# A two-block transformer kernel: the delta rule's triangular inverse by doubling block sizes on TensorE, and the recurrences issued in small steps

## The chip, the cores and the metric

The kernel runs on one core of a Trainium2 chip. The metric is device time in microseconds (us) of one execution. A core has TensorE (matrix products), VectorE (DVE), ScalarE (ACT) and GpSimd (POOL), which each work through a queue of their own in order, and SyncE (SP), whose queue here issues most DMAs. They wait for each other by semaphores.

## The reference

Input x is 1024 tokens of width 1024, in float32. Two blocks follow each other.

The first block has adaptive normalisation, a spatial gating unit beside top-k sparse attention, and a feed-forward of width 4096. The second projects its normalised input to `z` (the delta rule's features), `u` and gates, and then joins two recurrences and another such feed-forward:

```python
z = xn @ w_in[l]
z_rwkv, u, gates = jnp.split(z, [SHIFT_COLS, SHIFT_COLS + SSM_WIDTH], axis=-1)
z_mix = z_rwkv + (token_shift(z_rwkv) - z_rwkv) * mu_shift[l]
y_a = rwkv7_time_mix(z_mix, ...)      # the delta rule, 8 heads of 64
y_b = s5_ssm(u, ...)                  # S5: a complex diagonal state per group
g_a, g_b = jnp.split(jax.nn.sigmoid(gates), 2, axis=-1)
x = x + (g_a * y_a + g_b * y_b) @ w_out[l]
x = x + sq_relu_mlp(rmsnorm(x, norm2_g[l]), w_ff_up[l], w_ff_down[l])
```

The delta rule is a scan over tokens of a 64x64 state for each head:

```python
sk = jnp.einsum('bhvk,bhk->bhv', state, kk_t)
state = (state * w_t[:, :, None, :]
         - sk[..., None] * b_t[:, :, None, :]
         + v_t[..., None] * k_t[:, :, None, :])
y_t = jnp.einsum('bhvk,bhk->bhv', state, r_t)
```

The kernel computes it in chunks of 64 tokens. Within a chunk the effect of the tokens on each other is a strictly triangular 64x64 matrix for each head, and the chunk needs the inverse of one plus this matrix. That inverse is the subject of the change.

## The kernel before

**Dense products.** Every large product keeps float32 accuracy by splitting both operands into a high and a low part: `mm3` issues three matmuls of 128x512 (L66, L68, L69; called dense products below). After the first of them it calls `next(self.weave, None)`, so that a generator hung there emits one of its steps between the matmuls. Weights come through `load_w`: a 512 KB DMA on SP's queue into `wraw`, a cast by ACT and a subtraction by POOL into `whl`.

**Stages.** The sequence is worked in two halves of 512 tokens. For each, `sequences(h, ...)` computes the second block's input projection (`in2`) over 4352 columns, among it the delta rule for four tiles of 128 tokens (`rwkv(tt)`, two chunks of 64 tokens and eight heads each). In the first half the first block's feed-forward for the second half of the tokens comes next, then `merge`, which reads S5's and the delta rule's results back from DRAM (`yin`) and multiplies them by `w_glu` and `w_rwkv_proj`. In the second half seven eighths of the first half's last feed-forward stand between `sequences` and `merge`.

**The delta rule's tile.** `rwkv(tt)` loads its features (zw, zk, zr, zv), forms decays with two small products (L1271, L1272), normalises the keys (L1296), and forms the 64x64 matrices MM (L1326). Before the change it then inverts 32x32 blocks: MM's blocks go to DRAM (`lt_d`) and come back as L with one block on each partition, 31 steps of two VectorE operations (L1387 and L1389) run the substitution, the result goes through DRAM again (`tt_d`) into TT, VectorE transposes it (TI, L1401), and two small products (L1405, L1411) join two 32x32 inverses to one of 64x64. Products with the inverse (L1422) and with the state (L1436 to L1471) follow, a normalisation (L1483 to L1491), four transposes (L128), the gate G, and a store to `y_d`.

**S5.** `s5_steps(h)` is a generator: input products (L1721), rotations and scans on VectorE (up to L1736), copies to `s5t`, output products (L1764 and L1766) with weights of its own from DRAM (`s5w`), `y` by ACT (L1769) and a store to `y_d`. In the first half it hangs on `weave` in the last blocks of the first feed-forward, in the second in `in2`.

**The order.** A scheduler simulates a timeline and puts each engine's instructions into an order that is fixed when the kernel is built. Its priorities follow the order in which the code emits them; what stands in `with self.urgent()` goes ahead. In the kernel before, a delta tile is emitted whole, between two parts of `in2`.

Of the kernel before, what the change touches and what calls it, by code (L numbers as in the profile page):

```python
# [34 lines left out]
class Kernel:  # L35
# [64 lines left out]
    def load_w(self, w, k0, nk, c0, n, spare=None):  # L100
# [18 lines left out]
        return [(hl[:, 0, k, :], hl[:, 1, k, :]) for k in range(nk)]  # L119

# [741 lines left out]
    def ffn(self, hT, w_up, w_down, blocks=range(8), acc=None, gain=None, weave=None, spare=None):  # L862
# [6 lines left out]
        for fb in blocks:  # L869
            if fb == 5 and weave:  # L870
                next(weave)
            if fb == 6 and weave:
                self.weave = weave
# [44 lines left out]
        if weave:  # L918
            for _ in weave:
                pass  # L920
        return G, acc, ss

    def sequences(self, h, xT, s5=None):

        if h:
            self.in2(h, xT, 1792, 2304, True)
            s5 = self.s5_steps(h)
            next(s5)
            self.in2(h, xT, 0, 768)
# [27 lines left out]
    def run(self):  # L957
# [132 lines left out]
        after = self.ffn(hT, I["w_ff1"][0], I["w_ff2"][0], gain="G2", weave=self.s5_steps(0))  # L1090
# [79 lines left out]
    def rwkv_setup(self):  # L1170
# [55 lines left out]
    def rwkv(self, tt):  # L1226
# [18 lines left out]
        def ps512():  # L1245
            return self.tp.tile([P, 512], F32, name="tp")
# [624 lines left out]
```

## Time and profile before

| | before |
|---|---|
| median of 3 runs | 3047.42 us (3038.46 to 3047.6) |
| profiled execution, its own time | 3063.16 us |
| its span, first to last instruction | 3061.4 us |
| TensorE busy | 2831.0 us (92%) |
| VectorE, ACT, POOL busy | 1745.7, 1245.3, 1460.9 us |
| mean granted TensorE clock | 0.96 |

Times inside the execution count from the span's start. A busy time is the sum of an engine's instructions, overlaps counted once. The granted clock is 1.00 at TensorE's upper level (2.4 GHz) and 0.5 at its lower (1.2 GHz); a stretch's figure is the mean. An idle stretch of an engine is put down to what released the instruction that ended it. The length that a matmul's row shows is a modelled end, so its cost within a stream is read from the distance between starts.

### The profile page before, as it was taken

The numbers are of one execution on the slowest core, as the hardware profiler recorded it, in microseconds if no ns is written. First come the engines' busy times: TensorE is split into PE (matmuls) and PEld (weight loads), VectorE is DVE, ScalarE is ACT, GpSimd is POOL, SyncE is SP. The second block draws the span as 40 slices with busy tenths as digits, with TensorE's granted clock in tenths as the row PEclk, the third lists the DMA queues.
The fourth block names the chain that finished last, engine by engine and source line by source line (L and its number), as shares of the span: only waits on it lengthen the run. The fifth ranks groups of instructions, "written<-read, shape, count | busy, mean of one in ns | idle before, by whom it ended". The sixth has DMA issues, their size and how long they took to land.

```text
span 3061.4 us, 42378 instructions
## 1 busy us (share of the span) xinstructions
PE 2831.0 (92%) x15600; PEld 2337.1 (76%) x15600; DVE 1745.7 (57%) x3752; ACT 1245.3 (41%) x2121; POOL 1460.9 (48%) x1285
## 2 busy tenths in 40 slices
PE   6977998999998899889989999998899999999998
PEld 5865776787887777667777888887777778888887
DVE  5699569999946944445563563433655634332122
ACT  4545555444455333343333443332433333433333
POOL 4665544544445743434433465443343435454444
PEclk9988999999999999899999999999999999999999
DMA  7445332222224555333225484653323235442232
GB/s 252 136 130 178 124 118 64 90 79 69 73 84 148 179 164 152 103 86 90 76 84 147 147 274 123 178 147 107 81 92 90 82 90 155 141 131 97 97 97 83
DMA packets 301504, 370.22 MB, mean 121 GB/s; under 512 B 70936, under 2 KB 209902, under 8 KB 301040
## 3 DMA queue, kind: packets, MB, share of 16 engines
q1 hardware_dynamic: 293296, 351.75, 37.9%
q10 hardware_dynamic: 8000, 15.76, 1.5%
q8 instruction: 123, 2.02, 0.3%
q14 instruction: 85, 0.70, 0.1%
HBM read 315.80 MB, written 51.65 MB: 120 GB/s over the span
## 4 chain that ended last, share of the span: by engine, by line
PE 57%; DVE 27%; DMA 8%; issue 3%; ACT 2%; SPq 2%; POOL 1%; ACTq 0%; POOLq 0%; DVEq 0%
PE mm L66 16%; PE mm L68 16%; PE mm L69 16%; DVE junk L669 4%; DMA L<-lt_d 3%; DVE T L1389 2%; DVE Ttmp L1387 2%; DVE topk L680 2%; PE tp L128 1%; DVE acc L902 1%; DVE score L643 1%; DVE p L746 1%; DMA TT<-tt_d 1%; DVE p L735 1%; PE tp L764 1%
## 5 line engine op out<-in xcount | busy, mean ns | idle before, releaser
L118 POOL TENSOR_TENSOR whl<-wraw,whl 128x512 fp32r<-128x512 f32 (+1 forms) x836 | 1134.7, 1382 | 1255.7 <-ACT whl L116 1187.1
L66 PE MATMUL mm<-hT,whl 128*128 128x512 f32 x1760 | 699.1, 398 | 21.6 <-DVE acc L902 13.5
L68 PE MATMUL mm<-hT,whl 128*128 128x512 f32 x1760 | 701.6, 400 | 0.0
L69 PE MATMUL mm<-hT,whl 128*128 128x512 f32 x1760 | 694.8, 397 | 3.9 <-POOL whl L118 3.9
L116 ACT CAST whl<-wraw 128x1024 fp32r<-128x1024 f32 (+1 forms) x418 | 435.1, 1042 | 541.5 <-PE mm L69 389.7
L66 PE MATMUL mm<-whl,hT 128*128 128x512 f32 (+1 forms) x1584 | 614.6, 402 | 42.9 <-DVE acc L902 18.5
L68 PE MATMUL mm<-whl,hT 128*128 128x512 f32 (+1 forms) x1584 | 625.6, 396 | 0.4 <-POOL whl L118 0.4
L69 PE MATMUL mm<-whl,hT 128*128 128x512 f32 (+1 forms) x1584 | 614.3, 396 | 0.9 <-DVE hT L61 0.9
L66 PEld LDWEIGHTS mm<-hT,whl 128*128 128x128 f32 x1760 | 336.1, 191 | 97.2 <-DVE acc L902 15.2
L69 PEld LDWEIGHTS mm<-hT,whl 128*128 128x128 f32 x1760 | 336.3, 191 | 73.7 <-POOL whl L118 5.0
L66 PEld LDWEIGHTS mm<-whl,hT 128*128 128x128 f32 x1584 | 305.2, 193 | 112.2 <-DVE acc L902 22.2
L68 PEld LDWEIGHTS mm<-hT,whl 128*128 128x128 f32 x1760 | 336.1, 191 | 66.3 <-issue 0.9
L68 PEld LDWEIGHTS mm<-whl,hT 128*128 128x128 f32 x1584 | 305.9, 193 | 60.7 <-issue 1.2
L69 PEld LDWEIGHTS mm<-whl,hT 128*128 128x128 f32 x1584 | 303.3, 192 | 62.2 <-DVE hT L61 1.8
L902 DVE TENSOR_TENSOR acc<-mm,acc 128x512 f32<-128x512 f32 x240 | 160.6, 686 | 189.2 <-PE mm L69 188.7
L61 DVE TENSOR_TENSOR hT<-sm,hT 128x512 fp32r<-128x512 f32 x112 | 94.4, 846 | 265.2 <-ACT hT L60 264.5
L881 ACT ACTIVATE sm<-mm 128x512 f32<-128x512 f32 x128 | 76.5, 598 | 273.1 <-PE mm L69 267.3
L669 DVE TENSOR_SCALAR_CACHE_REDUCE junk<-score,topk 128x640 uint8<-128x640 f32 (+4 forms) x192 | 179.5, 941 | 1.8
L1387 DVE TENSOR_TENSOR Ttmp<-L,T 128x60 f32<-128x60 f32 (+24 forms) x248 | 77.8, 314 | 95.5 <-DMA L<-lt_d 88.1
L60 ACT CAST hT<-sm 128x512 fp32r<-128x512 f32 x144 | 89.3, 620 | 31.0 <-DVE sm L1835 28.3
L764 PE MATMUL tp<-pT,vhl 128*128 128x256 f32 x288 | 64.1, 310 | 25.0 <-ACT pT L760 7.4
L743 ACT ACTIVATE p<-p,nm 128x128 f32<-128x128 f32 (+7 forms) x64 | 49.6, 778 | 91.4 <-DVE nm L739 60.5
(470 smaller groups left out, 3489.2 us busy)
## 6 DMA issues: line engine op xcount, KB each, us to landing
wraw<-w_ff SPq DMA_DIRECT2D x128, 512.0 KB
wraw<-w_in SPq DMA_DIRECT2D x100, 512.0 KB
wraw<-w_ff_up SPq DMA_DIRECT2D x64, 512.0 KB
wraw<-w_ff_down SPq DMA_DIRECT2D x64, 512.0 KB
wraw<-w_ada SPq DMA_DIRECT2D x32, 512.0 KB
wraw<-w_out SPq DMA_DIRECT2D x32, 512.0 KB
raw<-w_ada SPq DMA_DIRECT2D x16, 512.0 KB
x_d<-acc ACTq DMA_DIRECT2D x16, 512.0 KB
```

The lines of the kernel that those rows point to most:

```text
L60: self.nc.scalar.copy(hi, src)
L61: (engine or self.nc.gpsimd).tensor_tensor(lo, src, hi.bitcast(F32), op=OP.subtract)
L66: nc.tensor.matmul(ps, a[0], b[0], start=start, stop=False)
L68: nc.tensor.matmul(ps, a[0], b[1], start=False, stop=False)
L69: nc.tensor.matmul(ps, a[1], b[0], start=False, stop=stop)
L116: nc.scalar.copy(hl[:, 0], raw)
L118: nc.gpsimd.tensor_tensor(hl[:, 1, s], raw[:, s], hl[:, 0, s].bitcast(F32), op=OP.subtract)
L669: V.tensor_scalar(junk[:, :n], sel, value, 0.0, op0=op, op1=OP.add, accum_out=cnt)
L764: nc.tensor.matmul(o, self.vhl[(s0 + i) // 4][:, (s0 + i) % 4, kv, :], t[:, x, 256 * i:256 * i + 256], start=(s0 + i + x == 0), stop=(s0 + ...
L881: nc.scalar.activation(r, ps, AF.Relu)
L902: nc.vector.tensor_tensor(d, pss[j], d, op=OP.add)
L1387: V.tensor_tensor(tmp[:, :n, :w], L[:, j:j + 1, j + 1:].to_broadcast([P, n, w]), T[:, :n, j:j + 1].to_broadcast([P, n, w]), op=OP.mult)
```

## The change

The inverse is no longer done by substitution. Masks `joins` for the block widths 1, 2, 4, ... 32 are built once. Starting from inverses of 2x2 blocks, five doublings each compute Y = MM times S, masked to the blocks that are joined, and then S (the inverse so far) and its transpose St by two further products, `each` being sixteen 64x64x64 products, one for each head and chunk. VectorE takes Y out of PSUM with the mask, ACT copies S and St. Both DRAM bounces and TI go.

`rwkv` becomes a generator with `yield` between its steps, and `delta(h)` chains the four tiles. It hangs on `weave`, ahead of S5 in the first half: `in2` from column 1792 (2304 in the second half) and the feed-forward behind it emit one step at each dense product. S5 of the second half now hangs on all of `in2` up to column 1792, and `drain` emits what is left before the merge.

The diff, cut to its core (most of the added `yield` lines are left out, they stand between the groups of instructions of `rwkv` that the listing above shows; line numbers of the kernel after are 5 higher here up to the delta rule and up to 30 higher behind it):

```diff
                 nc.gpsimd.tensor_tensor(hl[:, 1, s], raw[:, s], hl[:, 0, s].bitcast(F32), op=OP.subtract)
         return [(hl[:, 0, k, :], hl[:, 1, k, :]) for k in range(nk)]
+
+    def drain(self):
+
+        for _ in self.weave:
+            pass
...
-    def ffn(self, hT, w_up, w_down, blocks=range(8), acc=None, gain=None, weave=None, spare=None):
+    def ffn(self, hT, w_up, w_down, blocks=range(8), acc=None, gain=None, spare=None):
...
         for fb in blocks:
-            if fb == 5 and weave:
-                next(weave)
-            if fb == 6 and weave:
...
                     down(0, jj)
                     down(1, jj)
-        if weave:
-            for _ in weave:
-                pass
         return G, acc, ss
 
-    def sequences(self, h, xT, s5=None):
-
-        if h:
-            self.in2(h, xT, 1792, 2304, True)
-            s5 = self.s5_steps(h)
-            next(s5)
-            self.in2(h, xT, 0, 768)
-            self.weave = s5
-            self.in2(h, xT, 768, 1792)
-            for _ in s5:
-                pass
-        else:
-            self.in2(h, xT, 0, 1024, True)
-            self.weave = s5
-            self.in2(h, xT, 1024, 1792)
-            for _ in s5:
-                pass
+    def sequences(self, h, xT, s5):
+
+
+        self.in2(h, xT, *((1792, 2304) if h else (0, 512)), True)
+        self.weave = s5
+        self.in2(h, xT, *((0, 1792) if h else (512, 1792)))
+        self.drain()
+        self.weave = chain(self.delta(h), iter(()) if h else self.s5_steps(0))
+        self.in2(h, xT, 2304 if h else 1792, 4352)
+
+    def delta(self, h):
         with ExitStack() as st:
             self.rwkv_pools(st)
             for tt in range(4 * h, 4 * h + 4):
-                self.rwkv(tt)
-        self.in2(h, xT, 2304 if h else 1792, 4352)
+                yield from self.rwkv(tt)
 
 
...
@@ -1087,7 +1078,8 @@
         self.residual(1, None, rows, ss, lambda tt: I["x"][0, tt * P:(tt + 1) * P, :])
         self.sequences(0, xT, s5)
         *_, hT = self.norm_T(self.scaled_rows(rows, rstd=self.ssx_rstd(1)), self.s2, self.sh2)
-        after = self.ffn(hT, I["w_ff1"][0], I["w_ff2"][0], gain="G2", weave=self.s5_steps(0))
+        after = self.ffn(hT, I["w_ff1"][0], I["w_ff2"][0], gain="G2")
+        self.drain()
         ys = self.merge_in(0)
         self.residual(1, *after, lambda tt: self.x_d[tt], False)
         mT = self.merge(0, *ys)
...
-        self.sequences(1, xT)
+        self.sequences(1, xT, self.s5_steps(1))
         *_, hA = hA
         w = I["w_ff_up_2"][0], I["w_ff_down_2"][0]
         self.ffn(hA, *w, range(7), os)
+        self.drain()
...
-        self.eye32 = c.tile([P, 8, 32], F32, name="eye32")
-        nc.gpsimd.memset(self.eye32, 0.0)
-        for g in range(4):
-            nc.gpsimd.affine_select(self.eye32[32 * g:32 * g + 32], self.eye32[32 * g:32 * g + 32],
-                                    pattern=[[-4, 8], [1, 32]], compare_op=OP.not_equal, fill=-1.0, base=-g,
-                                    channel_multiplier=0)
+
+        self.joins = c.tile([P, 7, 64], F32, name="joins")
+        nc.gpsimd.memset(self.joins, 0.0)
+        for ch in range(2):
+            q = self.joins[64 * ch:64 * ch + 64]
+            for x in range(6):
+                w = 1 << x
...
+            up = q[:, 6].rearrange("p (b u) -> p b u", u=2)[:, :, 1:2]
+            nc.gpsimd.affine_select(up, up, pattern=[[-2, 32], [0, 1]], compare_op=OP.not_equal, fill=1.0, base=0,
+                                    channel_multiplier=1)
+        nc.vector.tensor_tensor(self.joins, self.joins, self.eye2[:, None].to_broadcast([P, 7, 64]), op=OP.add)
         self.state = self.stp.tile([P, 4, 64], F32, name="state")
         nc.vector.memset(self.state, 0.0)
-        self.lt_d = [self.dram.tile([32, 32, 32], F32, name=f"lt_d{t}") for t in range(8)]
-        self.tt_d = [self.dram.tile([32, 8, 4, 32], F32, name=f"tt_d{t}") for t in range(8)]
 
     def rwkv_pools(self, st):
         self.rk = self.pool("rk", st=st)
         self.ew = self.pool("ew", 4, st=st)
         self.TT = self.rk.tile([P, 8, P], F32, name="TT")
         self.nc.vector.memset(self.TT, 0.0)
-        self.TI = self.rk.tile([P, 8, 32], F32, name="TI")
-        self.nc.vector.memset(self.TI, 0.0)
 
...
@@ -1326,15 +1334,29 @@
                     nc.tensor.matmul(ps[:, c], BK[r, hh // 2, 2 * c:2 * c + 2, :].rearrange("p x t -> p (x t)"),
                                      PR[r, :, hh // 2, 64 * c:64 * c + 64], start=True, stop=True)
                 V.tensor_tensor(MM[:, hh + e], ps, self.mask2[:, None].to_broadcast([P, 2, 2, 64]), op=OP.mult)
-
-        lt = rk.tile([P, 8, 32], F32, name="ltc")
-        for b in range(4):
-            r = slice(32 * b, 32 * b + 32)
-            V.tensor_copy(lt[r], MM[r, :, b // 2, 0, 32 * (b % 2):32 * (b % 2) + 32])
-        for b in range(4):
-            nc.sync.dma_start(self.lt_d[tt][8 * b:8 * b + 8].rearrange("h j i -> j h i"), lt[32 * b:32 * b + 32])
-        L = rk.tile([P, 32, 32], F32, name="L")
-        nc.sync.dma_start(L, self.lt_d[tt].rearrange("b j i -> b (j i)")[None].to_broadcast([4, 32, 1024]))
+            yield from range(2)
+
+
+        S, St, Y = (rk.tile([P, 8, 64], F32, name=n) for n in ("S", "St", "Y"))
+
+        def join(x):
+            return self.joins[:, x, None, :].to_broadcast([P, 8, 64])
+
+        def each(ps, a, b):
+
+            for i in range(8):
+                for c, q in chunks:
+                    nc.tensor.matmul(ps[q, i * 64:i * 64 + 64], a[c][q, i], b[q, i], start=True, stop=True)
+
+        M = [MM[:, :, c, 0, :] for c in range(2)]
+        eye = self.eye2[:, None, :].to_broadcast([P, 8, 64])
+        for c, q in chunks:
+            V.tensor_tensor(M[c][q], M[c][q], eye[q], op=OP.subtract)
+        for c, q in chunks:
+            V.tensor_tensor(St[q], M[c][q], join(6)[q], op=OP.mult)
+        ps = ps512()
+        each(ps, M, eye)
+        V.tensor_tensor(S, ps.rearrange("p (h d) -> p h d", h=8), join(0), op=OP.mult)
 
         PQ = rk.tile([P, 8, 2, 64], F32, name="PQ")
...
@@ -1377,42 +1403,25 @@
         V.tensor_tensor(W, W, bc(self.lnb), op=OP.add)
         V.tensor_tensor(W, W, k4(pg), op=OP.mult)
         V.tensor_tensor(G1, k4(pg), bc(self.lnw), op=OP.mult)
-
-        T = rk.tile([P, 8, 32], F32, name="T")
-        tmp = rk.tile([P, 8, 32], F32, name="Ttmp")
-        nc.gpsimd.tensor_copy(T, self.eye32)
-        for j in range(31):
-            n = j // 4 + 1
-            w = 31 - j
-            V.tensor_tensor(tmp[:, :n, :w], L[:, j:j + 1, j + 1:].to_broadcast([P, n, w]),
-                            T[:, :n, j:j + 1].to_broadcast([P, n, w]), op=OP.mult)
-            V.tensor_tensor(T[:, :n, j + 1:], T[:, :n, j + 1:], tmp[:, :n, :w], op=OP.subtract)
-        for cg in range(4):
-            nc.sync.dma_start(self.tt_d[tt][:, :, cg, :], T[32 * cg:32 * cg + 32])
-        TT, TI = self.TT, self.TI
-        for c in range(2):
-            nc.gpsimd.memset(TT[64 * c:64 * c + 32, :, 64 * c + 32:64 * c + 64], 0.0)
-        for r in range(4):
-            nc.sync.dma_start(TT[32 * r:32 * r + 32, :, 32 * r:32 * r + 32],
-                              self.tt_d[tt][8 * r:8 * r + 8].rearrange("h m g i -> (m g) h i"))
-
-        for c in range(2):
-            r = slice(64 * c, 64 * c + 32)
-            V.transpose(TI[r], TT[r, :, 64 * c:64 * c + 32])
-        pz = ps512()
-        for i in range(8):
-            for c, q in chunks:
-                nc.tensor.matmul(pz[q, i * 32:i * 32 + 32], MM[q, i, c, 0, :], TI[q, i, :], start=True, stop=True)
-        Z = rk.tile([P, 8, 32], F32, name="Z")
-        nc.scalar.copy(Z, pz[:, :256].rearrange("p (h j) -> p h j", h=8))
-        po = ps512()
-        for i in range(8):
-            for c, q in chunks:
-                nc.tensor.matmul(po[64 * c:64 * c + 32, i * 32:i * 32 + 32], Z[q, i, :], TT[q, i, 64 * c + 32:64 * c + 64],
-                                 start=True, stop=True)
-        for c in range(2):
-            r = slice(64 * c, 64 * c + 32)
-            nc.scalar.copy(TT[r, :, 64 * c + 32:64 * c + 64], po[r, :256].rearrange("p (h i) -> p h i", h=8))
+        yield from range(2)
+
+        TT = self.TT
+        for x in range(1, 6):
+            ps = ps512()
+            each(ps, M, S)
+            V.tensor_tensor(Y, ps.rearrange("p (h d) -> p h d", h=8), join(x), op=OP.mult)
+            yield from range(3)
+            ps, pst = ps512(), ps512()
+            each(pst, (Y, Y), St)
+            pst = pst.rearrange("p (h d) -> p h d", h=8)
+            if x < 5:
+                each(ps, (St, St), Y)
+                nc.scalar.copy(S, ps.rearrange("p (h d) -> p h d", h=8))
+                nc.scalar.copy(St, pst)
+            else:
+                for c, q in chunks:
+                    nc.scalar.copy(TT[q, :, q], pst[q])
+            yield from range(3)
 
         X = rk.tile([P, 8, 64], F32, name="X")
         for hg in range(2):
...
+        yield from range(8)
         po = ps512()
         for kt in range(4):
...
+        yield from range(12)
         for kt in range(4):
             TO = self.s5_w(self.toep_d[:, 8 * kt:8 * kt + 8])
             OU = self.s5_w(self.out_d[:, 8 * kt:8 * kt + 8])
```

What it moves, first on TensorE in one tile of the delta rule. Before (`TI`, `TT`, `Z` are the tiles of the old join, `mm` rows are dense products):

```order
L69 MATMUL mm<-hT,whl 128x512
L66 MATMUL mm<-hT,whl 128x512
L68 MATMUL mm<-hT,whl 128x512
L1405 MATMUL tp<-TI,MM 64x32 x16
L69 MATMUL mm<-hT,whl 128x512
...
L1411 MATMUL tp<-TT,Z 32x32 x16
L69 MATMUL mm<-hT,whl 128x512
```

The same place after (L1349 is `each`):

```order
L1397 MATMUL tp<-zw,wgu 128x128 x4
L1400 MATMUL tp<-zr,blk 128x512
L1349 MATMUL tp<-S,MM 64x64 x16
L69 MATMUL mm<-hT,whl 128x512
...
L66 MATMUL mm<-hT,whl 128x512
L1349 MATMUL tp<-St,Y 64x64 x16
L1349 MATMUL tp<-Y,St 64x64 x16
L68 MATMUL mm<-hT,whl 128x512
...
L68 MATMUL mm<-hT,whl 128x512
L1349 MATMUL tp<-S,MM 64x64 x16
L69 MATMUL mm<-hT,whl 128x512
```

Two runs in each tile, 21 dense products apart, became runs and pairs of runs with 22 or 23 dense products between them (the stretches marked by "...").

Second, TensorE at the end of S5's first half. Before (`s5t` and `u` are S5's operands):

```order
L69 MATMUL mm<-hT,whl 128x512
L1766 MATMUL tp<-s5t,s5w 128x64
L1764 MATMUL tp<-u_15188,s5w 128x64
...
L1764 MATMUL tp<-u_15188,s5w 128x64
L1766 MATMUL tp<-s5t,s5w 128x64
L66 MATMUL mm<-hT,whl 128x512
L68 MATMUL mm<-hT,whl 128x512
```

The same place after (`whl,hT` with hT as the moving operand belongs to the feed-forward's down product, `hT,whl` behind S5 to the merge):

```order
L68 MATMUL mm<-whl,hT 128x512
L69 MATMUL mm<-whl,hT 128x512
L1783 MATMUL tp<-s5t,s5w 128x64
L1781 MATMUL tp<-u_15504,s5w 128x64
...
L1781 MATMUL tp<-u_15504,s5w 128x64
L1783 MATMUL tp<-s5t,s5w 128x64
L66 MATMUL mm<-hT,whl 128x512 x4
L68 MATMUL mm<-hT,whl 128x512
```

S5's output products, which had dense products of the feed-forward among them and 147 behind them, now stand behind the last of these, with the merge's first ones right behind. The input products (L1721, now L1737) moved too: 96 dense products of the feed-forward are left behind them.

Third, TensorE at the end of the eighth tile. Before:

```order
L68 MATMUL mm<-hT,whl 128x512
L69 MATMUL mm<-hT,whl 128x512
L128 MATMUL tp<-ident,ew 128x128 x4
L66 MATMUL mm<-hT,whl 128x512
L68 MATMUL mm<-hT,whl 128x512
```

After:

```order
L69 MATMUL mm<-whl,hT 128x512
L1431 MATMUL tp<-PQ,TT 128x128 x8
L1446 MATMUL tp<-MM,X 64x64 x8
L1454 MATMUL tp<-TBK,X 64x64 x4
...
L1472 MATMUL tp<-XV,MM 64x64 x16
L1478 MATMUL tp<-state,ew 64x64 x8
L1485 MATMUL tp<-state,ew 64x64 x8
L1478 MATMUL tp<-state,ew 64x64 x8
L133 MATMUL tp<-ident,ew 128x128 x4
L66 MATMUL mm<-hT,whl 128x512 x4
L68 MATMUL mm<-hT,whl 128x512
```

The tile's last products, which had dense products between them and 144 behind them, now follow each other, and the merge's first dense products follow them.

## Rows read from the trace of the kernel before

**Rows 1.** The page, part 1: engines, busy us, share, instructions.
```profile
PE 2831.0 (92%) x15600; PEld 2337.1 (76%) x15600; DVE 1745.7 (57%) x3752; ACT 1245.3 (41%) x2121; POOL 1460.9 (48%) x1285
```

**Rows 2.** Stages: stretch, its length, busy us (instructions) by engine, granted clock, DMA.
```profile
1160.00:1660.00 500.00, 453.87 (x3174) 368.62 (x3175) 260.99 (x554) 183.34 (x297) 194.92 (x157) 0.94 0.33 96
2020.00:2520.00 500.00, 462.25 (x3181) 375.80 (x3180) 256.07 (x553) 176.47 (x284) 194.15 (x155) 0.95 0.34 96
2800.00:2900.00 100.00, 100.00 (x443) 82.81 (x442) 20.35 (x27) 37.01 (x50) 50.19 (x37) 1.00 0.29 95
```

**Rows 3.** Waits of TensorE in 1160:1660; us in total, times, longest.
```profile
PE tp L1405 <- DVE TI L1401: 21.7, 4, 9.5
PE mm L66 <- DVE acc L902: 14.0, 2, 7.6
PE tp L1271 <- ACT zw L1266: 6.5, 1, 6.5
```

**Rows 4.** Waits of TensorE in 2020:2520.
```profile
PE tp L1405 <- DVE TI L1401: 21.0, 4, 7.0
PE mm L66 <- DVE acc L902: 13.5, 3, 6.4
```

**Rows 5.** The page, part 5: groups on VectorE; busy, mean ns, idle before.
```profile
L902 DVE TENSOR_TENSOR acc<-mm,acc 128x512 f32<-128x512 f32 x240 | 160.6, 686 | 189.2 <-PE mm L69 188.7
L1387 DVE TENSOR_TENSOR Ttmp<-L,T 128x60 f32<-128x60 f32 (+24 forms) x248 | 77.8, 314 | 95.5 <-DMA L<-lt_d 88.1
```

**Rows 6.** TensorE in order of time, old join: start us, us, line, shapes, [idle before].
```profile
1608.36 1.49 PE L1405 MATMUL tp<-TI,MM 64*64 64x32 f32 x32 [1.47 <-DVE TI L1401]
1609.78 0.50 PE L66 MATMUL mm<-hT,whl 128*128 128x512 f32 x1
```

**Rows 7.** TensorE in order of time, a run of 64x64 products.
```profile
1203.20 0.39 PE L69 MATMUL mm<-hT,whl 128*128 128x512 f32 x1
1203.51 1.15 PE L1363 MATMUL tp<-XV,MM 64*64 64x64 f32 x32
1204.59 1.16 PE L1371 MATMUL tp<-zw,wgu 128*128 128x128 f32 x8
```

**Rows 8.** TensorE in order of time, two runs in a row.
```profile
1265.75 1.15 PE L1451 MATMUL tp<-XV,TBK 128*64 128x64 f32 x32
1266.73 1.10 PE L1459 MATMUL tp<-XV,MM 128*64 128x64 f32 x32
1267.77 0.62 PE L1464 MATMUL tp<-state,ew 64*64 64x64 f32 x13
```

**Rows 9.** TensorE in order of time, runs on four quadrants.
```profile
1263.30 0.69 PE L1436 MATMUL tp<-MM,X 64*64 64x64 f32 x32
1263.82 0.65 PE L1443 MATMUL tp<-TBK,X 64*64 64x64 f32 x32
```

**Rows 10.** S5's end in the first half, in order of time: TensorE, ACT, VectorE.
```profile
1675.86 5.50 PE L1721 MATMUL tp<-u,s5w 128*64 128x64 f32 x128 [4.33 <-DMA s5w<-in_d]
...
1708.01 2.11 ACT L1754 COPY s5t<-xs 64x1024 f32<-64x1024 f32 x2 [13.45 <-DVE xs L1736]
...
1732.11 0.83 ACT L1769 ACTIVATE y<-tp 128x256 f32<-128x256 f32 x2 [2.74 <-PE tp L1766]
...
1748.26 4.39 DVE L1789 TENSOR_TENSOR hT<-yin,hT 128x512 fp32r<-128x512 f32 x4 [0.62 <-DMA yin<-y_d]
```

**Rows 11.** The eighth tile's end: TensorE, VectorE, SP's queue, VectorE.
```profile
2484.08 1.95 PE L1422 MATMUL tp<-PQ,TT 128*128 128x128 f32 x16
2489.59 0.69 PE L1436 MATMUL tp<-MM,X 64*64 64x64 f32 x32
...
2508.26 0.69 DVE L1491 TENSOR_TENSOR ew<-ew,rs 128x512 f32<-128x512 f32 x1 [2.33 <-POOL rs L78]
...
2519.39 1.77 SPq L1784 DMA_DIRECT2D yin<-y_d  x4
...
2524.78 1.10 DVE L1789 TENSOR_TENSOR hT<-yin,hT 128x512 fp32r<-128x512 f32 x1 [7.90 <-ACT hT L1788]
```

More of the change, by code (lines that the diff above doesn't have):

```diff
@@ L2 @@
 from contextlib import ExitStack
-from itertools import zip_longest
+from itertools import chain, zip_longest
 import concourse.bass as bass
@@ L1264, in rwkv @@
                               self.z_d[h][2][:, :, tok.start + 64 * c:tok.start + 64 * c + 64])
+        yield from range(4)
         nc.scalar.activation(zw[0:64, 0, :], zw[0:64, 0, :], AF.Tanh)
         nc.scalar.activation(zw[:, 1, :], zw[:, 1, :], AF.Sigmoid)
+        yield from range(2)
         pw, pa = ps512(), ps512()
@@ L1293, in rwkv @@
         nc.scalar.activation(sq, kk, AF.Square)
+        yield from range(6)
         pss = ps512()
@@ L1299, in rwkv @@
         nc.gpsimd.tensor_tensor(inv, inv, self.mhalf[:, :8], op=OP.pow)
+        yield from range(4)
         pi = ps512()
@@ L1303, in rwkv @@
                              inv[:, i:i + 1].to_broadcast([P, 64]), self.ident, start=True, stop=True)
+        yield
         V.tensor_tensor(kk, kk, k4(pi), op=OP.mult)
@@ L1328, in rwkv @@
                 V.tensor_tensor(MM[:, hh + e], ps, self.mask2[:, None].to_broadcast([P, 2, 2, 64]), op=OP.mult)
-        lt = rk.tile([P, 8, 32], F32, name="ltc")
-        for b in range(4):
-            r = slice(32 * b, 32 * b + 32)
-            V.tensor_copy(lt[r], MM[r, :, b // 2, 0, 32 * (b % 2):32 * (b % 2) + 32])
-        for b in range(4):
-            nc.sync.dma_start(self.lt_d[tt][8 * b:8 * b + 8].rearrange("h j i -> j h i"), lt[32 * b:32 * b + 32])
-        L = rk.tile([P, 32, 32], F32, name="L")
-        nc.sync.dma_start(L, self.lt_d[tt].rearrange("b j i -> b (j i)")[None].to_broadcast([4, 32, 1024]))
+            yield from range(2)
+        S, St, Y = (rk.tile([P, 8, 64], F32, name=n) for n in ("S", "St", "Y"))
[14 more added lines that the diff above has]
+        V.tensor_tensor(S, ps.rearrange("p (h d) -> p h d", h=8), join(0), op=OP.mult)
         PQ = rk.tile([P, 8, 2, 64], F32, name="PQ")
@@ L1345, in rwkv @@
         V.tensor_copy(PQ[:, :, 0, :], ps.rearrange("p (h d) -> p h d", h=8))
+        yield from range(2)
         ps = ps512()
@@ L1351, in rwkv @@
             nc.scalar.copy(XV[r, c], ps[r].rearrange("p (h d) -> p h d", h=8))
+        yield from range(2)
         for c in range(2):
@@ L1357, in rwkv @@
             nc.scalar.copy(TBK[:, c], ps)
+            yield from range(2)
         pq = ps512()
@@ L1365, in rwkv @@
         nc.scalar.copy(PQ[:, :, 1, :], pq.rearrange("p (h d) -> p h d", h=8))
+        yield from range(2)
         pg, pb = ps512(), ps512()
@@ L1413, in rwkv @@
-        for c in range(2):
-            r = slice(64 * c, 64 * c + 32)
-            nc.scalar.copy(TT[r, :, 64 * c + 32:64 * c + 64], po[r, :256].rearrange("p (h i) -> p h i", h=8))
+        yield from range(2)
+        TT = self.TT
[15 more added lines that the diff above has]
+            yield from range(3)
@@ L1428, in rwkv @@
                 nc.scalar.copy(XV[q, c, hs], px[q, :, 1, :])
+            yield from range(2)
         RT, FT, HC = ew(), ew(), ew()
@@ L1438, in rwkv @@
             V.tensor_tensor(RT[:, :, q], pr[c][:, :256].rearrange("p (k t) -> p k t", k=4), PR[:, 1, :, q], op=OP.add)
+        yield from range(2)
         pf = [ps512(), ps512()]
@@ L1446, in rwkv @@
                             self.eye2[:, None, :].to_broadcast([P, 4, 64]), op=OP.add)
+        yield from range(2)
         ph = ps512().rearrange("p (c x) -> p c x", c=2)
@@ L1453, in rwkv @@
             nc.scalar.copy(HC[:, :, q], ph[:, c].rearrange("p (k d) -> p k d", d=64))
+        yield from range(2)
         py = [ps512(), ps512()]
@@ L1460, in rwkv @@
                                  skip_group_check=True)
+        yield
         for c, q in chunks:
@@ L1476, in rwkv @@
             self.state = new
+            yield from range(3)
         yt, y2t = ew(), ew()
@@ L1491, in rwkv @@
         V.tensor_tensor(y, y, r[:, :, None].to_broadcast([P, 8, 64]), op=OP.mult)
+        yield from range(8)
         po = ps512()
@@ L1724, in s5 @@
                 nc.scalar.copy(X[:, x, 4 * kt:4 * kt + 4, 1:65], ps[:, x])
+            yield from range(2)
         co, si = self.rot[:, 0], self.rot[:, 1]
@@ L1755, in s5 @@
         y = self.s5c.tile([P, 32, 64], F32, name="y5")
-        yield
+        yield from range(12)
         for kt in range(4):
```

8 lines of the change are left out of this document (7 added, 1 removed).

## The prediction, made before the result was known

> **What bounds the kernel now.** I read the page first: TensorE is busy for 92% of the span and no other engine for more than 57% [rows 1]. So time is won only where TensorE stands idle or runs slowly, and lost wherever it gets more to do. The view of stages comes next. In an undisturbed stage of 100 us TensorE is busy for all of it and issues 443 products, 0.2257 us each [rows 2]; this is the price of one dense 128x512 product at the upper clock level. The two stages that hold the delta rule's eight tiles (four in each) differ: they are 500 us long with 453.87 and 462.25 us busy, at a granted clock of 0.94 and 0.95 [rows 2]. The other stages are nearly full, so these two are what the change can win.
>
> The view of waits says what the 46.1 and 37.8 us of idle time are. The first product that joins two 32x32 inverses (L1405) waits for VectorE's transposes of TI: 21.7 and 21.0 us, four times in each stage. Dense products wait for the addition to `acc` (L902), 14.0 and 13.5 us, and that addition stands on VectorE behind the inverse. The start of the first tile (L1271) waits 6.5 us [rows 3, 4]. The chain behind the TI wait is in the page: 248 pairs of small VectorE operations, L1387 alone 77.8 us busy with 88.1 us of waiting for the bounce through `lt_d` [rows 5]. The change takes out precisely this.
>
> **What goes.** (a) Idle time: 46.1 + 37.8 = 83.9 us; I let 4 us of short waits stay and count 80. (b) Clock: 0.94 and 0.95 of 500 us mean 60 + 50 = 110 us at the lower of the two levels (1.2 instead of 2.4 GHz), where a busy microsecond does half the work. If all 83.9 us of idle time lay in these 110, the loss is (110 - 84) / 2 = 13 us; if none did, 55. I take the middle, 34, since neither row says where the slow stretches lie. (c) The old joining products: L1405's 32 instructions run from 1608.36 to the next dense product at 1609.78, 1.42 us [rows 6], and L1411's half as many columns some 0.7; 2.1 us by 8 tiles is 17. Together 131 us. VectorE's loop and the 104 DMAs that bounced L and TT cost nothing of their own beyond these waits.
>
> **What comes.** Each tile now issues 15 runs of 16 products 64x64x64, one for eye, five for S and nine for Y and St. fp32 takes two instructions for each, so a run is 32 instructions. Nothing in the old kernel is nearer than L1363: same 32 instructions, 64x64 by 64 columns, on two quadrants. The last dense product starts at 1203.20, the run at 1203.51 instead of 1203.43, the next group at 1204.59 [rows 7]: 1.08 us and 0.09 to switch in, 1.17 for a run that stands alone. Two such runs in a row (L1451, L1459, start of L1464) are 0.98 and 1.04 apart [rows 8], so a pair is 2.1. By the order two of a tile's 15 runs (eye, the first S) stand next to other small runs, the other four S and the last Y stand alone among dense products, and eight make four pairs (St,Y with Y,St): 2 x 1.0 + 5 x 1.17 + 4 x 2.1 = 16.3 us, by 8 tiles 130. Bounds: L1436, whose 32 instructions use all four quadrants, gives 0.52 us to the next run [rows 9], hence about 0.57 x 15 x 8 = 68 below, and L1405's 1.42 gives 170 above. I take L1363, because a product of the new run also reads and writes the same two quadrants.
>
> A rule of the Trainium skill speaks against small runs among dense ones: "TensorEngine Tiling (Array Packing)", Key Properties, says that a change of the tiling mode drains TensorE. The row bears it out in kind, 0.31 us instead of 0.23 from the dense start to the small one, and so at 0.09 us a switch, which stands in my 1.17 already. If each of some 80 entries cost the whole 0.39 us that a dense product's row shows as its length, the sum would be some 24 us worse.
>
> The evacuations between runs are hidden if they end before the next run. The order puts some 22 dense products, 22 x 0.2257 = 5.0 us, between a run and the one that needs it. One needs a VectorE operation of 128x512 (0.69 us as L902's, [rows 5]) or two ACT copies, some 1.4 us by the same measure; what else stands in the queues has the remaining 3.6 us. So I count nothing. Net of the two stages: 130 - 131 = -1 us.
>
> **The two new ends.** The steps are now issued one per dense product, and there are not enough dense products behind them.
>
> End A, S5 in the first half. Before, 147 dense products of the feed-forward stand behind its output products. Now the delta rule comes first in the same queue of steps, S5's input products (old L1721) come 96 dense products before the end of the feed-forward, and all 64 output pairs and then the merge come with no dense work left. Old rows: L1721 ends at 1681.36, VectorE's rotations and ACT's copy to s5t end at 1710.1, 28.8 us later [rows 10]; 96 x 0.2257 = 21.7 cover it, so TensorE waits 7. The last y (ACT L1769) ends at 1732.94; the y_d store, the yin load and the two casts give the first merge operand at 1749.4, 16.4 us [rows 10], and the merge's first product needs exactly that. A weight load that stands between them on SP's queue is not there in the new order, so I take 15. Clock after the stall 2. The old wait of S5's start for its weights, 4.3 us [rows 10], is filled by steps now. A: 7 + 15 + 2 - 4 = 20 (14 to 25).
>
> End B, the eighth tile. Before, 144 dense products are left when its last transposes run. Now from L1422's product with TT on to the merge none is left. Old rows: L1422 starts at 2484.08, the normalised y is ready at 2508.95 [rows 11], 24.9 us. Part of this is queueing behind dense products, which goes: L1422's run ends at 2486.0 and L1436 starts at 2489.6, 3.6 us later, of which the copies of X need some 0.9, so 2.7; with the like before the outer products and the last state product I put it at 8. That leaves 17 us, in which TensorE works some 7 itself (seven short runs at about 1). So 10 us idle; and if the merge's yin load, which is released by this tile's buffers, starts only then, 2519.39 to 2525.88 [rows 11], 6.5 more. 10 to 16.5; I take 12, and 2 for the clock: 14.
>
> **Sum.** -131 + 130 + 20 + 14 = +33 us. The profiled execution took 3063.16 us, which gives 3096. It stands 15.7 us above the median of the runs shown, 3047.42; in their terms 3080, 1.1% slower.
>
> **Rivals.** R1, evacuations late: the queues of VectorE and ACT hold S, Y and St behind additions to `acc` and casts, and more than 5.0 us pass. For it: VectorE is half busy there (261 of 500 us [rows 2]). Against: 496 operations and their waits leave it. At 0.5 us late for 80 joins it is 40 us, and some 5 more of lower clock: 3125. It decides from 5.0 us between run and evacuation on.
>
> R2, faster: the two quadrants of a run work side by side, as the four of L1436 do at 16 ns an instruction against L1363's 34 [rows 7, 9]. Then the runs cost 68 instead of 130: 3018. For it: the pace seen in L1436. Against: L1451 and L1459 show 31 ns too, with two quadrants. It decides if a run takes under 0.8 us. The Trainium skill's same page and section says that tiles load weights and multiply in parallel, which is this rival.
>
> R3, no change: the ends A and B are covered, because S5 and the eighth tile run further ahead of the dense products than I count, or the loads start earlier. Without the 34 us: 3046. Against it: the order shows no dense product behind either.
>
> **Chances.** My forecast 0.60, R1 0.14, R3 0.16, R2 0.10. Under 0.3%, some 9 us, a measurement of this kernel can't be told from no change. Slower: of the forecast 0.51, R1 0.14, R3 0.03, which is 0.68. Same: 0.06 + 0.09 + 0.02 = 0.17. Faster: 0.03 + 0.04 + 0.08 = 0.15. Range: below to R3's 3046 and a little beyond, since the clock's bound (55 instead of 34) takes off 21 more, 3040; above, A and B at their upper ends add 9 and a part of R1, and the clock's lower bound (13) 21, to 3120. Cases of slower hold most; the likeliest one's own range is 3055 to 3105.
>
> **What would show it.** In the profile of the changed kernel: no wait of TensorE on VectorE in the delta stages and a granted clock near 1.00 there; runs of L1349 some 1.1 us apart in a pair; a wait of some 7 us before the first S5 output product (L1783) at the end of the first feed-forward and one of some 15 before the merge's first product; some 10 us or more of short waits from L1431 to the last transposes of the eighth tile. I am wrong if the two delta stages get shorter by more than 25 us in the same dense work (R2, or a larger clock term), if L1349 waits for S, Y or St (R1), or if the two ends show waits under 5 us.

## The result: 2.7% slower

The changed kernel takes 3128.02 us (median of 4 runs, 3121.4 to 3135.34), the kernel before 3047.51 in the same comparison: a ratio of 1.0271, 95% interval 1.0247 to 1.0295. The forecast was slower, 3080 with 3040 to 3120; the time lies 48 us above it and 8 above the range. The profiled execution's span is 3133.6 us, 72.2 longer than before. It took 3135.34 us, 7.3 above the kernel's median, and the one before 3063.16, some 15.7 above its own: what follows explains the 72 us of these two executions, while the medians are 80.5 apart.

The page of the kernel after, part 1, and its stages (columns as in [rows 1, 2]); the last line, by itself, is the kernel before, where its S5 setup stands:

```profile
PE 2949.4 (94%) x18928; PEld 2436.4 (78%) x18928; DVE 1610.7 (51%) x3287; ACT 1281.5 (41%) x2178; POOL 1459.1 (47%) x1295
```

```profile
1160.00:1660.00 500.00, 497.47 (x4505) 404.81 (x4504) 172.33 (x288) 189.79 (x298) 190.85 (x143) 0.99 0.28 85
2100.00:2590.00 490.00, 490.00 (x4545) 400.38 (x4544) 176.26 (x280) 184.84 (x290) 185.53 (x138) 1.00 0.27 83
992.00:1080.00 88.00, 77.49 (x340) 63.74 (x339) 77.37 (x218) 27.29 (x45) 56.51 (x62) 0.91 0.50 165
```

```profile
992.00:1070.00 78.00, 70.07 (x293) 56.46 (x293) 75.95 (x215) 27.67 (x47) 56.43 (x62) 0.96 0.53 172
```

In the delta rule's stages the change did what it was counted on for: 497 of 500 and 490 of 490 us busy at 0.99 and 1.00, against 454 and 462 of 500 at 0.94 and 0.95 [rows 2]. The price is there too. TensorE is busy for 118 us more than before and idle for 46 less. One pair of runs, TensorE in order of time (start us, us, line, shapes), and the groups of L1349 over the whole execution (busy, mean ns | idle before them):

```profile
1200.47 0.39 PE L66 MATMUL mm<-hT,whl 128*128 128x512 f32 x1
1200.79 1.15 PE L1349 MATMUL tp<-St,Y 64*64 64x64 f32 x32
1201.78 1.10 PE L1349 MATMUL tp<-Y,St 64*64 64x64 f32 x32
1202.81 0.50 PE L68 MATMUL mm<-hT,whl 128*128 128x512 f32 x1
1203.14 0.39 PE L69 MATMUL mm<-hT,whl 128*128 128x512 f32 x1
```

```profile
L1349 PE MATMUL tp<-S,MM 64*64 64x64 f32 x1280 | 45.9, 221 | 0.0
L1349 PE MATMUL tp<-St,Y 64*64 64x64 f32 x1280 | 45.9, 221 | 0.0
L1349 PE MATMUL tp<-Y,St 64*64 64x64 f32 x1024 | 35.2, 218 | 0.0
L1349 PE MATMUL tp<-eye,MM 64*64 64x64 f32 x256 | 11.7, 223 | 0.0
```

The pair takes 2.02 us from its start to the next dense product, and no run waits for its operands. The two ends look as follows; first the waits of TensorE around the end of the first half's S5 (us in total, times, longest):

```profile
PE mm L66 <- ACT hT L1805: 15.2, 1, 15.2
PE mm L66 <- DVE acc L903: 6.2, 2, 4.8
PE mm L66 <- ACT whl L116: 3.1, 2, 2.3
PE tp L1737 <- DMA s5w<-in_d: 2.5, 1, 2.5
PE tp L1781 <- DMA s5w<-toep_d: 2.4, 1, 2.4
PE tp L1783 <- DMA s5w<-out_d: 0.8, 1, 0.8
```

The stages of that end, three stretches at the lower clock (the last of them lies elsewhere, in the delta rule, and comes up under e3 and e6), and TensorE in order of time at the end:

```profile
1773.00:1798.00 25.00, 21.44 (x125) 20.77 (x123) 10.40 (x10) 9.67 (x23) 10.40 (x17) 0.67 0.71 242
1798.00:1835.00 37.00, 19.76 (x80) 15.92 (x81) 9.95 (x12) 11.26 (x14) 5.49 (x4) 0.76 0.75 228
```

```profile
1764.50:1768.00 3.50, 3.50 (x8) 2.83 (x9) 3.50 (x2) 0.00 (x0) 2.68 (x2) 0.51 0.31 107
1781.60:1815.70 34.10, 16.93 (x71) 16.01 (x72) 11.93 (x11) 4.91 (x8) 5.01 (x10) 0.50 0.84 254
1286.60:1300.30 13.70, 12.93 (x49) 10.30 (x48) 11.35 (x18) 9.38 (x19) 8.29 (x6) 0.50 0.16 54
```

```profile
1774.32 0.39 PE L1783 MATMUL tp<-s5t,s5w 128*128 128x64 f32 x2
1774.55 0.39 PE L1781 MATMUL tp<-u,s5w 128*128 128x64 f32 x2
...
1782.71 1.09 PE L1781 MATMUL tp<-u,s5w 128*128 128x64 f32 x4 [2.42 <-DMA s5w<-toep_d]
...
1785.53 0.63 PE L1781 MATMUL tp<-u,s5w 128*128 128x64 f32 x2
1785.95 0.63 PE L1783 MATMUL tp<-s5t,s5w 128*128 128x64 f32 x2
...
1812.92 2.08 PE L66 MATMUL mm<-hT,whl 128*128 128x512 f32 x4 [15.24 <-ACT hT L1805]
```

The first half of S5's output products run 0.22 us apart, the second half 0.43: the granted clock has fallen to its lower level. It fell at 1781.6, within the wait of 2.42 us for S5's weights, and stayed there for 34.1 us. In these comes the wait of 15.24 us for y's way through DRAM. The end of the eighth tile:

```profile
2588.00:2618.00 30.00, 14.78 (x244) 12.32 (x244) 11.80 (x22) 9.94 (x15) 6.87 (x6) 0.71 0.29 84
```

```profile
2599.25 0.68 PE L1478 MATMUL tp<-state,ew 64*64 64x64 f32 x16 [1.06 <-DVE state L1489]
2606.03 1.08 PE L133 MATMUL tp<-ident,ew 128*128 128x128 f32 x4 [6.10 <-DVE ew L1506]
2615.16 2.08 PE L66 MATMUL mm<-hT,whl 128*128 128x512 f32 x4 [8.05 <-ACT hT L1805]
```

Half of these 30 us are idle: the normalisation and then the load of `yin`, both foreseen.

**Where the 72 us lie.** Every kernel issues 10080 dense products, mostly in the same sequence, so the time between the n-th and the m-th can be compared across traces. Worked out by counting L66, L68 and L69 in each (us; e6 and e10 are experiments below):

| dense products | before | after | e6 | e10 |
|---|---|---|---|---|
| 2784 to 3376 (S5's setup, start of the delta rule) | 176.8 | 187.6 | 190.0 | 185.0 |
| 3376 to 5424 (delta rule, S5 and end A) | 642.9 | 686.9 | 646.8 | 620.4 |
| 5424 to 8064 (second half's delta rule and end B) | 779.9 | 801.3 | 783.4 | 756.4 |

What is left lies ahead of the second block, where the code is the same: the changed kernel is some 4 us shorter there (988.2 against 992.4).

The two lower rows together can be split further. TensorE's busy time less half of what it was busy at the lower level is its work at the upper level; the other half is what the lower clock cost (us, from the start times and clock records of the traces):

| dense products 3376 to 8064 | before | after | e6 |
|---|---|---|---|
| work at the upper level | 1287 | 1412 | 1421 |
| idle | 93 | 55 | 8 |
| cost of the lower clock | 43 | 22 | 2 |

So the change brings 125 us of work, and takes away 38 of idle time and 21 of lower clock.

### The profile page after: what moved, and what is told of

Its sections match the earlier page's. It is cut to its first block, busy times and chain, and to the rows that moved or that the text cites. A ratio compares the mean times of both kernels' runs of the same rounds, so it can differ in the third digit from the quotient of the medians.

```text
span 3133.6 us, 48491 instructions
## 1 busy us (share of the span) xinstructions
PE 2949.4 (94%) x18928; PEld 2436.4 (78%) x18928; DVE 1610.7 (51%) x3287; ACT 1281.5 (41%) x2178; POOL 1459.1 (47%) x1295
## 5 line engine op out<-in xcount | busy, mean ns | idle before, releaser
L66 PE MATMUL mm<-hT,whl 128*128 128x512 f32 x1760 | 700.1, 399 | 42.4 <-ACT hT L1805 23.3
L68 PE MATMUL mm<-hT,whl 128*128 128x512 f32 x1760 | 696.2, 397 | 0.0
L69 PE MATMUL mm<-hT,whl 128*128 128x512 f32 x1760 | 692.1, 396 | 3.2 <-POOL whl L118 3.2
L66 PE MATMUL mm<-whl,hT 128*128 128x512 f32 (+1 forms) x1584 | 613.7, 400 | 24.3 <-DVE acc L903 7.2
L68 PE MATMUL mm<-whl,hT 128*128 128x512 f32 (+1 forms) x1584 | 626.5, 396 | 0.2 <-POOL whl L118 0.2
L69 PE MATMUL mm<-whl,hT 128*128 128x512 f32 (+1 forms) x1584 | 613.1, 394 | 0.0
L66 PEld LDWEIGHTS mm<-hT,whl 128*128 128x128 f32 x1760 | 335.6, 191 | 117.8 <-ACT hT L1805 23.9
L69 PEld LDWEIGHTS mm<-hT,whl 128*128 128x128 f32 x1760 | 335.0, 190 | 74.0 <-POOL whl L118 3.6
L68 PEld LDWEIGHTS mm<-hT,whl 128*128 128x128 f32 x1760 | 335.1, 190 | 69.2 <-issue 0.8
L66 PEld LDWEIGHTS mm<-whl,hT 128*128 128x128 f32 x1584 | 304.5, 193 | 90.1 <-DVE acc L903 9.0
L68 PEld LDWEIGHTS mm<-whl,hT 128*128 128x128 f32 x1584 | 304.9, 193 | 60.0 <-POOL whl L118 1.1
L69 PEld LDWEIGHTS mm<-whl,hT 128*128 128x128 f32 x1584 | 303.3, 192 | 60.4 <-issue 0.2
L1412 DVE TENSOR_TENSOR Y<-tp,joins 128x512 f32<-128x512 f32 x40 | 27.6, 689 | 193.4 <-PE tp L1349 193.4
```

What stands on the lines that cost most here:

```text
L66: nc.tensor.matmul(ps, a[0], b[0], start=start, stop=False)
L68: nc.tensor.matmul(ps, a[0], b[1], start=False, stop=False)
L69: nc.tensor.matmul(ps, a[1], b[0], start=False, stop=stop)
```

## The experiments

All kernels ran in comparison with the kernel before (3047.6 to 3050.8 us in these). T is the theory that the inverse by doubling, being longer in the order, bares the two ends; U that issuing in small steps does.

**e1: the new inverse alone**, in the kernel before.

```diff
-        for j in range(31):
-            n = j // 4 + 1
...
+        for x in range(1, 6):
+            ps = ps512()
+            each(ps, M, S)
...
```

> The kernel before with the inverse by doubling in place of the substitution, everything else issued as before (a delta tile emitted whole, no steps). Theory T (the longer inverse bares the ends): its order has delta tiles some 430 to 450 dense products apart instead of 370 to 390, S5's output products of the first half again behind the feed-forward's last dense product and tile 8 with no dense product behind it, so it is as slow as the changed kernel: 3110 to 3140 us, with waits of some 15 us before the first half's merge. Rival U (issuing in small steps bares the ends): without steps the ends stay covered and only the runs' 130 us against the waits' 130 remain: 3035 to 3060 us.

Measured 3142.89 us, ratio 1.0319 (1.0293 to 1.0345): even 15 us above the changed kernel, and 3 above T's range. Waits of TensorE around the first half's S5:

```profile
PE tp L1766 <- POOL s5t L1752: 21.7, 1, 21.7
PE mm L66 <- ACT hT L1788: 14.3, 1, 14.3
```

T holds and U falls: without any small step of the delta rule both waits of end A are there, and before the second half's merge there are waits of 6.1 and 8.4 us. Issuing in small steps, with all that moves with it, saves those 15 us.

**e2: the steps alone**, with the old inverse put back.

```diff
-        for x in range(1, 6):
...
+        for j in range(31):
...
+            if j % 2:
+                yield
...
+        yield from range(6)
+        pz = ps512()
```

> The changed kernel with the old inverse (substitution on VectorE, both bounces through DRAM) put back, issued in small steps. Theory T: the ends are covered again (its order has S5's output products at dense product 4951 of 5232 and tile 8's last transposes at 7680 of 7872), no wait before either merge; L1405's waits of about 5 us each stay, because its order puts 114 dense products between L1363 and it as before: 3030 to 3055 us. Rival U: steps bare the ends whatever the inverse: 3090 to 3130 us. A third reading: the steps hide the waits for TI: 2960 to 3010 us.

Measured 3048.01 us, ratio 0.9998 (0.9983 to 1.0013). T again: no bare end (no wait of TensorE above 1.7 us around end A, none around end B), no gain either. Waits in 2020:2520:

```profile
PE mm L66 <- DVE acc L903: 20.0, 5, 7.9
PE tp L1415 <- DVE TI L1410: 10.5, 3, 8.7
```

They are the old ones [rows 4], only divided in another way.

**e3: four quadrants.** Odd heads' Y and S go to the other half of the partitions.

```diff
-            each(ps, M, S)
+            pp = [ps512(), ps512()]
+            for i in range(8):
+                for c, q in chunks:
+                    d = chunks[c ^ (i & 1)][1]
+                    nc.tensor.matmul(pp[c][d, i // 2 * 64:i // 2 * 64 + 64], M[c][q, i], S[q, c ^ (i & 1), i // 2],
+                                     start=True, stop=True)
...
```

> The changed kernel; the odd heads' Y and S products write the other half of the partitions, so that the runs for Y (5 in a tile) and S (4) use all four quadrants and two PSUM banks, as L1436 does; one more small copy for each. If a run on four quadrants costs 0.52 us and one on two 1.05, TensorE does 9 x 0.5 x 8 = 36 us less; the order still has both ends bare, so 3085 to 3100 us. Rival (a run's price is its 32 instructions, not its quadrants): no change, 3120 to 3135 us.

Measured 3106.92 us, ratio 1.0198 (1.0169 to 1.0227), 21 less. A run on four quadrants:

```profile
1211.85 0.69 PE L1420 MATMUL tp<-S,MM 64*64 64x64 f32 x32
1212.47 0.50 PE L69 MATMUL mm<-hT,whl 128*128 128x512 f32 x1
```

0.62 us to the next product instead of the 1.08 of a run of the changed kernel that stands alone: the price does hang on the quadrants. This run also writes two PSUM banks, but that alone does not give the pace. In the changed kernel L1478's 64x64 products write two banks too, from two quadrants, and 13 instructions take 0.41 us, 31 ns each:

```profile
2597.04 0.62 PE L1478 MATMUL tp<-state,ew 64*64 64x64 f32 x13
2597.45 0.27 PE L1485 MATMUL tp<-state,ew 64*64 64x64 f32 x1
```

By the count of dense products the delta rule's two stretches (3376 to 5042 and 6220 to 7600) became 30 us shorter, 36 being expected. Some 6 of the 30 are not the quadrants': the changed kernel's profiled execution ran at the lower clock from 1286.6 to 1300.3, busy for 12.93 us, and e3's kept 1.00 there. That leaves some 24, near the 21 of the medians.

**e4: two doublings left out** (widths 8 and 16, so the inverse is not the whole one).

```diff
-        for x in range(1, 6):
+        for x in (1, 2, 5):
```

> The changed kernel without the doublings from width 8 and 16 (6 of 15 runs of a tile; the inverse that it uses is not the whole one). The work left out is 6 x 1.05 x 8 = 50 us of TensorE. Theory T: the tiles get shorter too, its order has S5's output products of the first half at dense product 4903 of 5232 and tile 8's transposes at 7604 of 7872, so the two bare ends (47 and some 30 us) go as well: 2995 to 3020 us. Rival U (the ends come from the steps, not from the length of the inverse): only the 50 us, 3070 to 3085 us.

Measured 3018.82 us, ratio 0.9915 (0.9887 to 0.9943): 109 less, of which the runs explain 50. No wait above 1.0 us is left around end A:

```profile
PE mm L66 <- DVE acc L903: 1.0, 1, 1.0
PE mm L66 <- ACT whl L116: 0.9, 2, 0.5
```

T holds: a shorter inverse takes the two ends with it.

**e5: end A covered.** The merge of the first half multiplies the delta rule's part first, with S5's last steps still woven in.

```diff
-        self.drain()
-        ys = self.merge_in(0)
...
+        mT = self.merge(0, None, yr)
...
+            if step and not h:
+                self.drain()
+                y5, _ = self.merge_in(0)
```

> The changed kernel; the merge of the first half multiplies the delta rule's part (96 dense products) first, issued with S5's last steps still woven in, and S5's part after it. End A then has dense products beside S5's output products and behind its y. Theory T (end A costs 47 us by lying bare: 15 for y's way through DRAM, the rest waits and half clock around S5's output products): 25 to 45 us less, 3085 to 3103 us; end B unchanged. Rival (the dense products there merely move and the wait falls elsewhere): under 8 us less, 3120 to 3130 us.

Measured 3113.53 us, ratio 1.0212 (1.0195 to 1.0229): 14.5 less, between the two readings (25 to 45, and under 8). Waits of TensorE in 1710:1860:

```profile
PE mm L66 <- ACT hT L1811: 7.3, 1, 7.3
PE tp L1742 <- DMA s5w<-in_d: 6.5, 1, 6.5
PE mm L66 <- DVE acc L903: 5.0, 2, 4.8
```

The cover came only in part: of the 15 us for y's way through DRAM 7.3 are left, and S5's input weights come later. It shows that dense products there take time off end A; for its price see e6.

**e6: half runs.** The same products in runs of four heads.

```diff
-            ps = ps512()
-            each(ps, M, S)
-            V.tensor_tensor(Y, ps.rearrange("p (h d) -> p h d", h=8), join(x), op=OP.mult)
-            yield from range(3)
...
+            for hs in parts:
+                s = slice(hs[0], hs[-1] + 1)
+                ps = ps512()
+                each(ps, M, S, hs)
+                V.tensor_tensor(Y[:, s], hds(ps)[:, s], join(x)[:, s], op=OP.mult)
+            yield from range(5)
...
```

> The changed kernel with the same products of the inverse, each run split into two half runs of four heads with evacuations of their own (five steps instead of three behind each). Its order has the delta tiles some 366 dense products apart instead of 440, S5's output products of the first half at dense product 4921 of 5232 and tile 8's last transposes at 7632 of 7872. Theory T: TensorE's 134 us of runs stay, both ends are covered: 3128 - 47 - 30 = 3051, with 16 more groups of evacuations some 3045 to 3065 us. Rival (the ends' waits come back inside the tiles as waits for Y, S and St, since half runs stand closer): 3090 to 3130 us.

Measured 3082.63 us, ratio 1.0114 (1.0097 to 1.0131), 45 less; 18 above T's upper end, since T's sum took off 77 us for the two ends, where the traces show 58. With the ends covered the waits are gone and nothing comes back in the tiles:

```profile
1160.00:1660.00 500.00, 498.46 (x4793) 401.48 (x4791) 187.85 (x327) 200.36 (x352) 187.23 (x142) 1.00 0.30 86
2020.00:2520.00 500.00, 500.00 (x4799) 403.08 (x4798) 194.19 (x334) 194.89 (x345) 183.00 (x137) 1.00 0.28 87
```

This prices the ends, in the table above: 801.3 - 783.4 = 18 us for B, and 686.9 - 646.8 = 40 for the rows with A. Some 6 of the 40 lie in the stretch from 1286.6 to 1300.3, where e6 keeps 1.00, so 34 are left for A. In both differences e6's own runs count against the ends: split in halves, they are 9 us more work (1421 against 1412).

**e7 and e8: half runs on four quadrants**, St taken out by ACT (e7) or by VectorE (e8).

```diff
-                        nc.scalar.copy(St[q, hs[0]:hs[-1] + 1], hds(pp[b])[q, 4:4 + 4])
+                        V.tensor_copy(St[q, hs[0]:hs[-1] + 1], hds(pp[b])[q, 4:8])
```

> Half runs as in e6, and Y's and S's runs on four quadrants as in e3, S and St of a half sharing two PSUM banks (ACT takes S and St out). Ends covered by its order (4951 of 5232, 7672 of 7872). Theory T: e6's time less what four quadrants gave in e3 (21 us and some 9 more in the delta stages): 3015 to 3035 us, faster than the kernel before. Rival (10 to 13 dense products, 2.3 to 2.9 us, between the runs don't cover eight ACT copies of some 0.4 us): waits of about 1 us at each of 80 runs, 3060 to 3110 us.

> As e7, but VectorE takes St out instead of ACT. If ACT's copies were the bound of e7, 10 to 30 us less than e7; if nothing waits in e7, the same within 8 us. Theory T: 3010 to 3035 us.

Measured 3074.42 us (ratio 1.0080, 1.0063 to 1.0096) and 3087.54 (1.0131, 1.0116 to 1.0146). Both miss: four quadrants give only 8 us over e6, and VectorE is worse than ACT, not better. In e7 TensorE is busy for 497.29 of 500 us in the first stage, so its waits are not the reason. The order breaks the work into more pieces among dense products: between 3376 and 8064 TensorE goes from a dense product to a small one or back 352 times in the changed kernel, 382 in e3, 448 in e6, 468 in e7 and 530 in e8. At some 0.1 us each (the pair above shows 0.09 on the way in and 0.10 on the way back) that is an estimate of 9 us between e3 and e7, where the work at the upper level differs by 13, and of 6 between e7 and e8, where it differs by 18. So it takes up a part of the gain; the rest stays open.

**e9: S5's setup put back**, in e7.

```diff
-        self.in2(h, xT, *((1792, 2304) if h else (0, 512)), True)
+        self.in2(h, xT, *((1792, 2304) if h else (0, 1024)), True)
...
-        self.in2(h, xT, *((0, 1792) if h else (512, 1792)))
+        self.in2(h, xT, *((0, 1792) if h else (1024, 1792)))
```

> As e7, but S5's setup in the first half is woven into columns 1024 to 1792 as in the kernel before instead of 512 to 1792. What stands at dense product 3376 came some 11 us later in the changed kernel than before; if S5's setup among the earlier dense products costs that (weights cast late, half clock), 8 to 12 us less than e7: 3062 to 3067 us. If the place of the setup costs nothing, as e7, 3070 to 3078 us.

Measured 3064.40 us, ratio 1.0040 (1.0028 to 1.0053): 10 less than e7, as expected. From dense product 2784 to 3376 the profiled execution takes 178.5 us, e7's 190.4. The earlier place of S5's setup is a cost of its own; it shows in the rows 992:1080 and, before, 992:1070 above, with a clock of 0.91 instead of 0.96.

**e10: the old inverse in steps, with room.** In e2:

```diff
-        yield from range(6)
+        yield from range(64)
         pz = ps512()
...
-        yield from range(3)
...
```

> e2 (old inverse, small steps) with 64 steps instead of 6 between the substitution's end and L1405, and none behind it in the tile; by its order L1405 stands 184, 158, 128, 128, 212, 134, 120 and 132 dense products behind L1374 instead of about 115 to 130. If the waits for TI are only a matter of the place in the queue, three of the eight waits go and the lower clock behind them: 10 to 25 us less than e2, 3023 to 3038 us, which beats both kernels. If VectorE, held by the wait for L, only delays the dense products' own additions instead, as e2: 3040 to 3055 us.

Measured 3020.00 us, ratio 0.9893 (0.9874 to 0.9911): 1.1% faster than before and 3.5% than the changed kernel. Its stages, and the longest waits of the first, with the last line from the second:

```profile
1160.00:1660.00 500.00, 476.76 (x3406) 387.21 (x3405) 239.68 (x545) 187.10 (x303) 206.33 (x161) 0.98 0.38 106
2020.00:2520.00 500.00, 473.57 (x3244) 384.19 (x3244) 244.09 (x558) 185.06 (x288) 200.92 (x158) 0.98 0.34 100
```

```profile
PE mm L69 <- POOL whl L118: 6.6, 2, 5.3
PE mm L66 <- DVE acc L903: 6.1, 5, 2.5
PE tp L1415 <- DVE TI L1410: 4.5, 2, 3.8
PE tp L1415 <- DVE TI L1410: 3.2, 3, 2.0
```

The waits for TI that were the reason for the new inverse mostly go (7.7 us of 42.7 are left) by a later place of L1405 in TensorE's queue, with no more products on TensorE. The two stages still have some 50 us of idle time, now for other operands.

## Why the prediction was wrong, step by step

*What goes, and the evacuations.* Right: the idle time and the lower clock of the two stages are gone but for the 13.7 us at 1286.6, and L1349 never waits, so R1 does not happen. The lower clock cost 43 us before, against the 34 booked between bounds of 13 and 55.

*What comes.* Nearly right: 2.02 us for a pair and 1.08 for a run alone, as its rows had it (those for a pair, L1451 and L1459, are 128x64 products; the price is the same). The switch from dense to small shows 0.32 us between starts (1200.47 to 1200.79) and 0.23 otherwise, the 0.09 of the sum. The Trainium skill's rule on the tiling mode ("TensorEngine Tiling (Array Packing)", Key Properties) is borne out in kind, and not only on the way in. The step back shows 0.33 us (1202.81 to 1203.14), another 0.10 that the sum did not have: at nine entries in each tile some 7 us, so the runs cost some 137 instead of 130.

With the ends covered (e6) the two stretches are 3.9 and 3.5 us longer than before, where the sum had -1, and 9 us are the price of the half runs. So the sum's core, a trade of waits against runs that comes out near nothing, held in the profiled executions. By the medians it may be worse: e6 is 35 us slower than the kernel before, of which S5's setup is some 10. The profiled execution of the kernel before stood 15.7 us above its median, and how much of that lies in these stages is not known.

*End B.* Near: 18 us against 14.

*End A.* The step that failed: "A: 7 + 15 + 2 - 4 = 20 (14 to 25)". In the same terms it cost some 36 (34 against e6). The first two were measured nearly as forecast, 6.2 (as waits for `acc` behind S5's operations on VectorE, not for s5t) and 15.24. What failed most is the term for the clock, 2 us. TensorE was busy for 16.93 of the 34.1 us at the lower level and for 3.5 more behind the second wait for `acc`, which costs half of these, some 10. S5's output products fell into it: 15.0 us for the second half from its first start to its end (0.8 of it a wait), where the first takes 6.3. The waits for S5's own weights (2.4, 0.8) and for late weights of the merge (3.1) had no term at all, and the old wait before S5's input products, booked as a gain of 4, only shrank from 4.3 to 2.5: 6.2 + 15.2 + 10 + 3.2 + 3.1 - 1.8 = 36. The forecast took the clock as something that follows the long wait; here it fell ahead of it, within one of the short ones.

*What the sum left out.* S5's setup moved to earlier dense products. It stood in the diff, and nothing was booked for it: 187.6 against 176.8 us in the table, 10 in e9.

By stretches, the rows of the two ends give 58 (34, 18 and the 6 at 1286.6) instead of 34, the stages +7 instead of -1, and the setup 11: 76 us, less the 4 ahead of the second block 72, the difference of the spans. The order had shown both ends in advance; their direction was right and the price of A was not. R2's mechanism exists (e3: 0.62 against 1.08 us), but not in the kernel as changed, whose runs stay on two quadrants. R3, covered ends, is e6, and it too is slower than before.

## What to carry to other kernels

Where TensorE is the bound, a chain on another engine that makes it wait is first to be given room in the order (e10: 28 us less for moved steps), and only then to be put on TensorE, where its whole time counts. A longer chain is paid twice if it runs up to the end of the work that covers it: count in the order how many dense products stand behind its last step, and price a bare end with the lower clock on the products in it, not only with its waits. Small products gain by using all four quadrants in whole runs (e3, 21 us); in half runs 8 us of that were left (e7).

## What the hardware showed that was not expected

The lower clock held while TensorE was busy. It fell within a wait of 2.4 us, after waits of 1.4 and 4.8 us in the 30 us ahead, and S5's 128x64 products, busy for 14.15 of the next 15.0 us, ran at 0.50 throughout. In the kernel before the same products stand next to dense ones without a wait and keep 1.00 (the second row, from the kernel before):

```profile
1782.70:1797.70 15.00, 14.15 (x64) 13.78 (x64) 9.52 (x8) 1.15 (x3) 4.16 (x7) 0.50 0.92 322
1713.90:1732.50 18.60, 18.60 (x145) 17.68 (x144) 0.70 (x1) 5.49 (x11) 5.37 (x4) 1.00 0.62 198
```

And 32 instructions of 64x64 by 64 columns take 1.08 us on two quadrants and 0.62 on four, from their start to the next dense product, in two kernels that differ in little else (the changed one and e3).
